# The gate projection of a linear-attention layer, from four passes of 512 columns to two blocks of 1024 columns with seven products on three of eight pairs

## The chip, the cores and the metric

The kernel is written for one Trainium2 chip and uses one of its cores. A core has five engines that matter here: TensorE (PE) multiplies matrices into a PSUM memory of eight banks, VectorE (DVE) and ScalarE (ACT) work on tiles in SBUF and PSUM, GpSimd (POOL) does small work and issues some of the DMAs, and SyncE (SP) issues the other DMAs. Each engine works through its own queue in order, and semaphores tie the queues together. The metric is the time of one execution on the device in microseconds (us). The kernel before took 2172.56 us as the median of three runs (2172.04 to 2177.0).

## The reference, cut to what matters

The program is a two-layer decoder on 256 positions of width 2048 in float32: a gated linear attention, a convolutional FFN, a block-sparse attention, and a second FFN. The change touches the first of these alone:

```python
xn = rms_norm(x, norm_w)
proj = xn @ w_in                       # 2048 -> q 1024, k 1024, v 2048, g 2048
q, k, v, g = jnp.split(proj, ...)
...                                    # decays, chunked linear attention -> o, 4 heads of 512
o = rms_norm(o, o_norm_w) * jax.nn.silu(g)      # the gate
return o.reshape(B, S, 2048) @ w_out
```

The gate is the last quarter of `proj`: 256 rows times a weight matrix of 2048 x 2048, whose result goes through SiLU and multiplies the normalized output of the attention.

## The kernel before, in words

**Products in three parts.** TensorE runs on a rounded float32 format. So that the result keeps float32's precision, each operand is split in a high and a low part, and each product is done three times: high times high, low times high, high times low. The activations are split once (`xw`). The weights come from HBM in tiles of 128 x 2048 (`wraw`, 1 MB each), and each half of 128 x 1024 is split when it is needed: ACT casts the high part (`whi`, line 150) and DVE subtracts to get the low part (`wlo`, line 152). A *step* is the work that TensorE does with one such half. `WeightStream.prefetch` emits the splits a few steps ahead of their use; `whi` and `wlo` live in three rotating buffers each (`parts`), and some of them in slots of a larger pool.

**Two ways to do a block.** `gemm_tok` is the plain way: 512 columns at a time, two accumulators in PSUM (one for each 128 rows), eight steps of 12 products of 512 columns each. `down` does 1024 columns at a time over eight *pairs* of 256 input features, and uses all eight PSUM banks. A plain pair there is two steps of 12 products. A pair that the table `ORDERS` marks with `+` is done by a Strassen-like scheme with seven block products in place of eight: 21 products of 512 columns in four steps (3, 6, 6 and 6). For such a pair DVE makes sums of the weights (`t13` and `t24`, lines 111 to 113), the sums are split too (3.5 halves in place of 2), and sums of the activations have to be there (`comb`). At the end of a block the partial results in the banks `p1` to `p8` are added up by one ACT copy and eight DVE additions. For names in `DIRECT` this is done between and after the last pairs, the tail: ACT copies `p1`, DVE adds `p6` and `p7`, then come the additions with `p2`, `p4`, `p5`, and after the second half of the tail those with `p3` and `p8`.

**The stage of the change.** The order is: values, keys (`down("k")`, one block, three of eight pairs by seven products), queries (two passes of `gemm_tok`), gate (four passes of `gemm_tok`, one for each head), then the output projection (`down("go")`). Inside the query and gate stages the attention itself is done: `gla_scores` (TensorE's `sT`) and `gla_values` (`o`) for each head. `after(n, job)` puts a job in front of the n-th next step. When a pass of the gate is done, ACT applies SiLU to the two accumulators, DVE multiplies with the normalized attention output and transposes 32 x 32 blocks (`z`), and GpSimd writes `z` to HBM and reads it back transposed (`turned`). Some steps later `gated` scales it (`g`), splits it (`go`) and, for pairs that the output projection does by seven products, makes operand sums (`comb`, lines 312 to 315); these four or five small operations are queued behind the split that was emitted last (`ws.behind()`).

**What sets the order.** The program is written with these jobs and due steps, and a scheduler then places the instructions of each engine's queue. So the order that the chip sees on each engine is that of the built program, of which the section on the change shows pieces.

## Time and profile before

| what | value |
|---|---|
| median of three runs | 2172.56 us (2172.04 to 2177.0) |
| the profiled execution, its own time | 2172.24 us |
| its span, first to last instruction | 2170.5 us |
| PE busy in the span | 2160.8 us |
| DVE, ACT busy in the span | 1639.0 us, 1294.7 us |
| TensorE's granted clock over the span | 1.00 |
| keys' block, 100.9 to 142.4 us: PE, DVE, ACT busy | all of it, 37.9, 26.5 us of 42.5 |
| gate stage with its attention, 203.0 to 290.3 us: PE, DVE, ACT busy | all of it, 51.0, 57.1 us of 87.3 |

The span is what the profiler records from the first to the last instruction; the execution's own time has 1.7 us around it. PE's busy time takes in overlapping, pipelined products, so that "busy" says that PE was not waiting, and how densely it works is read from the start of one product to the next. An idle time that the profile gives for an engine is the time just before an instruction, with the event that ended it.

### The profile page before, as it was taken

To read this page: it belongs to the slowest core of one execution; us is meant where nothing else is said; L and a number is where in the kernel's file an instruction comes from. 1 tells how busy PE (TensorE), PEld (TensorE's weight loads), DVE (VectorE), ACT (ScalarE), POOL (GpSimd) and SP (SyncE) were. 2 spreads that over 40 slices of the span, in tenths; PEclk is the share of its full clock that TensorE was granted. 3 is DMA by queue.
4 is the path that set the end of the run, shared out by engine and by line. 5 is a ranking of instruction groups with operands and counts; after the bars stand their busy time and mean duration, and the time that the engine had idled before them with its cause. 6 is when DMAs were issued, how large, how long until landed. Compare 5 with 4: busy or idle time off the path is not lost.

```text
span 2170.5 us, 27023 instructions
## 1 busy us (share of the span) xinstructions
PE 2160.8 (100%) x9681; PEld 1790.7 (83%) x9681; DVE 1639.0 (76%) x2274; ACT 1294.7 (60%) x1872; POOL 296.8 (14%) x448
## 2 busy tenths in 40 slices
PE   9999999999999999999999999999999999999999
PEld 7888888888888888888888888888888888888887
DVE  6785687667776767988977787676777776779987
ACT  6656665556555556555566676565656565656454
POOL 1011111111111111000022241011111111110000
PEclk9999999999999999999999999999999999999999
DMA  8566577677777777575676887676777778785655
GB/s 316 182 232 214 195 244 251 224 232 251 240 245 237 247 236 246 201 259 203 237 270 241 270 273 238 201 235 228 236 247 232 252 235 251 233 252 204 242 195 173
DMA packets 91480, 510.10 MB, mean 235 GB/s; under 512 B 13729, under 2 KB 14769, under 8 KB 41426
## 3 DMA queue, kind: packets, MB, share of 16 engines
q1 hardware_dynamic: 60722, 417.53, 55.2%
q0 software_dynamic: 30048, 90.28, 15.1%
q8 instruction: 75, 1.23, 0.2%
q10 hardware_dynamic: 576, 0.58, 0.1%
q14 instruction: 59, 0.48, 0.1%
HBM read 463.22 MB, written 45.11 MB: 234 GB/s over the span
## 4 chain that ended last, share of the span: by engine, by line
PE 94%; issue 3%; DMA 1%; ACT 0%; DVE 0%; SPq 0%; POOL 0%; DVEq 0%; POOLq 0%; ACTq 0%
PE acc L299 41%; PE p L353 31%; PE acc L302 20%; DMA w2s<-w2a 0%; PE hf L836 0%; DMA c<-rows 0%; PE sT L694 0%; PE o L711 0%; DMA wraw<-w_v 0%; PE s L949 0%; ACT whi L150 0%; DMA gn<-cst 0%; PE z L552 0%; PE s L947 0%; DVE wlo L152 0%
## 5 line engine op out<-in xcount | busy, mean ns | idle before, releaser
L152 DVE TENSOR_TENSOR wlo<-wraw,whi 128x1024 fp32r<-128x1024 f32 (+1 forms) x786 | 926.2, 1187 | 385.0 <-ACT whi L150 374.8
L150 ACT CAST whi<-wraw 128x1024 fp32r<-128x1024 f32 (+1 forms) x786 | 797.4, 1025 | 624.5 <-PE acc L299 394.7
L299 PE MATMUL acc<-whi,xw 128*128 128x512 f32 x3584 | 888.3, 390 | 2.4 <-ACT whi L150 2.1
L299 PEld LDWEIGHTS acc<-whi,xw 128*128 128x128 f32 x3584 | 671.4, 188 | 144.3 <-ACT whi L150 4.0
L302 PE MATMUL acc<-wlo,xw 128*128 128x512 f32 x1792 | 480.0, 389 | 0.0
L302 PEld LDWEIGHTS acc<-wlo,xw 128*128 128x128 f32 x1792 | 336.3, 188 | 69.9
L353 PE MATMUL p<-whi,hid 128*128 128x512 f32 x1078 | 288.1, 389 | 0.0
L353 PEld LDWEIGHTS p<-whi,hid 128*128 128x128 f32 x1078 | 202.2, 188 | 41.9
L353 PE MATMUL p<-wlo,hid 128*128 128x512 f32 x539 | 155.2, 389 | 0.0
L150 ACT CAST whi<-t 128x1024 fp32r<-128x1024 f32 x90 | 92.7, 1052 | 81.6 <-PE p L353 68.3
L780 POOL DMA_DIRECT2D upT<-turned x176 | 113.9, 654 | 144.8 <-DMA turned<-z 63.3
L299 PE MATMUL acc<-whi,xkv 128*128 128x512 f32 x512 | 127.9, 391 | 0.0
L774 POOL DMA_DIRECT2D turned<-z x44 | 34.1, 774 | 681.4 <-DVE z L770 618.0
L353 PEld LDWEIGHTS p<-wlo,hid 128*128 128x128 f32 x539 | 101.2, 188 | 21.1
L152 DVE TENSOR_TENSOR wlo<-t,whi 128x1024 fp32r<-128x1024 f32 x90 | 107.9, 1218 | 10.9 <-PE p L353 5.7
L353 PE MATMUL p<-whi,comb 128*128 128x512 f32 x360 | 116.1, 389 | 0.0
L789 ACT ACTIVATE au<-upT,cs 128x256 f32<-128x256 f32 x176 | 96.0, 595 | 23.8 <-DMA upT<-turned 23.7
L299 PEld LDWEIGHTS acc<-whi,xkv 128*128 128x128 f32 x512 | 94.6, 188 | 18.7
L793 DVE SCALAR_TENSOR_TENSOR au<-upT,cs,au 128x255 f32<-128x255 f32 x176 | 76.6, 470 | 12.8 <-ACT au L789 12.7
L795 DVE SCALAR_TENSOR_TENSOR au<-upT,cs,au 128x254 f32<-128x254 f32 x176 | 80.3, 476 | 0.0
L353 PEld LDWEIGHTS p<-whi,comb 128*128 128x128 f32 x360 | 67.5, 188 | 13.9
L302 PE MATMUL acc<-wlo,xkv 128*128 128x512 f32 x256 | 68.8, 390 | 0.0
(240 smaller groups left out, 1810.6 us busy)
## 6 DMA issues: line engine op xcount, KB each, us to landing
wraw<-w_up SPq DMA_DIRECT2D x176, 1024.0 KB, 5.3
wraw<-w_dn SPq DMA_DIRECT2D x88, 1024.0 KB, 4.9
turned<-z POOLq DMA_DIRECT2D x44, 512.0 KB, 3.5
upT<-turned POOLq DMA_DIRECT2D x176, 128.0 KB, 5.0
wraw<-w_g SPq DMA_DIRECT2D x16, 1024.0 KB, 5.0
wraw<-w_go SPq DMA_DIRECT2D x16, 1024.0 KB, 6.2
wraw<-w_kk SPq DMA_DIRECT2D x16, 1024.0 KB, 5.7
wraw<-w_kv SPq DMA_DIRECT2D x16, 1024.0 KB, 6.3
```

The lines of the kernel that those rows point to most:

```text
L150: one = nc.scalar.copy(hi[:, a:b], src[:, a:b])
L152: two = nc.vector.tensor_sub(lo[:, a:b], src[:, a:b], hi[:, a:b].bitcast(F32))
L299: T.matmul(ps[t], xs(kt)[:, x0 + 128 * t:x0 + 128 * t + 128], hi[:, c:c + 512], start=kt == 0 and x0 == 0, stop=False)
L302: T.matmul(ps[t], xs(kt)[:, 128 * t:128 * t + 128], lo[:, c:c + 512], start=False, stop=kt == KT - 1)
L353: T.matmul(p[n], x[xi], w[wi][:, 512 * f:512 * f + 512], start=n not in begun, stop=left[n] == 0)
L774: nc.gpsimd.dma_start(turned[J].rearrange("(a i) r q c -> (i r) a (q c)", a=4), z.rearrange("p (a q) t c -> p a (q t c)", a=4))
L780: nc.gpsimd.dma_start(f[32 * q:32 * q + 32].rearrange("p a (i c) -> p (a i) c", i=4), turned[J][:, :, q, :].rearrange("a r c -> r a c"))
L789: A.activation(au[:, i, :], t[:, i, :], AF.Identity, bias=col(cb + n), scale=col(cw + 2 * 2 * FT + n))
L793: V.scalar_tensor_tensor(au[:, i, 1:], t[:, i, :S - 1], col(cw + 2 * FT + n), au[:, i, 1:], op0=OP.mult, op1=OP.add)
L795: V.scalar_tensor_tensor(au[:, i, 2:], t[:, i, :S - 2], col(cw + n), au[:, i, 2:], op0=OP.mult, op1=OP.add)
```

## The change

The gate becomes a third user of `down`, as two blocks of 1024 columns. Pairs 1, 3 and 4 are done by seven products, after the plain pairs 0, 2 and 5; pairs 6 and 7 are the tail. The sums of the activations are those that the keys' block made (`x_sums`), which are kept. The function `gate` becomes `gate_rows`, which gets a finished tile in SBUF instead of an accumulator in PSUM. The due steps of the attention's scores and values move, so that they fall in plain pairs, where four PSUM banks are free, and those of `gated` move from 12 steps behind to 8 or 9. The weights of the gate are stored in the order of the new blocks.

```diff
+    "g": [_order("0 2 5 1+ 3+ 4+ | 6 7"), _order("0 2 5 1+ 3+ 4+ | 6 7")],
 }
-DIRECT = ("k", "mq")
+DIRECT = ("k", "mq", "g")
...
-    plan = [..., (w_qa, 2, 8192), (w_g, 4, 8192), (w_go, "go", None),
+    plan = [..., (w_qa, 2, 8192), (w_g, "g", None), (w_go, "go", None),
...
-    down("k", nrm.xs, {}, None, key_rows, {})
+    x_sums = {}
+    down("k", nrm.xs, x_sums, None, key_rows, {})
...
-            after(11 + 2 * i, lambda hd=hd: gla_scores(hd))
-            after(13 + 2 * i, lambda hd=hd: gla_values(hd))
+            after((10, 22)[g] + i, lambda hd=hd: gla_scores(hd))
+            after((12, 24)[g] + i, lambda hd=hd: gla_values(hd))
...
-    def gate(hd, ps):
-        z = fresh()
-        for t in range(2):
-            g = temp("tok", (128, 512))
-            A.activation(g, ps[t], AF.Silu, scale=nrm.col[:, t:t + 1])
-            V.scalar_tensor_tensor(g, heads[hd]["o"][:, t, :], heads[hd]["r"][:, t:t + 1], g,
-                                   op0=OP.mult, op1=OP.mult)
-            square(z, g, t)
-        return z
-
     fresh, square, through = turned("gates", GH)
-    for hd in range(GH):
-        z = gemm_tok(xs, 1, lambda ps: gate(hd, ps))
-        through(hd, z, [(12 + i, lambda f, c=2 * hd + i: gated(c, f)) for i in range(2)])
+    zg = {}
+
+    def gate_rows(t, hd, g):
+        if t == 0:
+            zg[hd] = fresh()
+        A.activation(g, g, AF.Silu, scale=nrm.col[:, t:t + 1])
+        V.scalar_tensor_tensor(g, heads[hd]["o"][:, t, :], heads[hd]["r"][:, t:t + 1], g, op0=OP.mult, op1=OP.mult)
+        square(zg[hd], g, t)
+        if t:
+            through(hd, zg[hd], [(8 + hd % 2 + i, lambda f, c=2 * hd + i: gated(c, f)) for i in range(2)])
+
+    down("g", nrm.xs, x_sums, None, gate_rows, {})
...
-        "w_g": _groups(win[:, 2 * KD + VD:], 512),
+        "w_g": _quads(win[:, 2 * KD + VD:], ORDERS["g"]),
```

A line is added at the top, so that the lines from 54 on stand one further down in the changed kernel, and those of the gate some more.

**First place: DVE's queue where the operands of the output projection's first pairs are made.** Before, this falls in the plain passes of the gate; these are the rows for head 1 (its third and fourth pair of columns, `go_2375` and `go_2397`).

```order
L152 TENSOR_TENSOR wlo_2339<-wraw_2239,whi_2338 128x1024
L152 TENSOR_TENSOR wlo_2355<-wraw_2239,whi_2354 128x1024
L152 TENSOR_TENSOR wlo_2379<-wraw_2273,whi_2378 128x1024
L314 TENSOR_TENSOR comb_2400<-g_2394 128x128
L312 TENSOR_TENSOR comb_2400<-g_2394 128x128
L428 TENSOR_TENSOR go_2375<-g_2372,go_2375 128x2x256
L313 TENSOR_TENSOR comb_2400<-comb_2400,g_2394 128x128
L428 TENSOR_TENSOR go_2397<-g_2394,go_2397 128x2x256
L315 TENSOR_TENSOR comb_2400<-g_2394,comb_2400 128x128
L152 TENSOR_TENSOR wlo_2409<-wraw_2273,whi_2408 128x1024
```

In the changed kernel the same work, here for head 0 (`go_2295`, `go_2309`), stands in the second block of the gate, between the splits and weight sums of its first two pairs with seven products.

```order
L153 TENSOR_TENSOR wlo_2277<-t13_2149,whi_2276 128x1024
L113 TENSOR_TENSOR t24_2272<-t13_2271,wraw_2082 128x512
L153 TENSOR_TENSOR wlo_2299<-t24_2150,whi_2298 128x1024
L315 TENSOR_TENSOR comb_2312<-g_2306 128x128
L114 TENSOR_TENSOR t24_2272<-wraw_2082,t24_2272 128x512
L313 TENSOR_TENSOR comb_2312<-g_2306 128x128
L429 TENSOR_TENSOR go_2295<-g_2292,go_2295 128x2x256
L153 TENSOR_TENSOR wlo_2321<-wraw_2082,whi_2320 128x512
L429 TENSOR_TENSOR go_2309<-g_2306,go_2309 128x2x256
L314 TENSOR_TENSOR comb_2312<-comb_2312,g_2306 128x128
L316 TENSOR_TENSOR comb_2312<-g_2306,comb_2312 128x128
L429 TENSOR_TENSOR comb_2317<-comb_2312,comb_2317 128x4x128
```

What moved: the small operations, which stood among splits of plain pairs, now stand among the splits and sums of `t13` and `t24`. Ahead of these rows DVE has `wlo_2254`, `t13_2271` and one scalar operation, and the half `whi_2330` comes next on ACT.

**Second place: ACT's queue for head 1's operands.** Before, with what each waits for:

```order
L617 ACTIVATE g_2372<-turned_2160,cs_82 128x256
L150 CAST whi_2378<-wraw_2273 128x1024 [waits DMAHW6_49,DVE_49,PE_49]
L617 ACTIVATE g_2394<-turned_2160,cs_82 128x256 x2
L428 CAST go_2375<-g_2372 128x2x256 [waits Activation_49]
L428 CAST go_2397<-g_2394 128x2x256 [waits Activation_49]
L150 CAST whi_2408<-wraw_2273 128x1024 [waits DVE_49,PE_49]
L428 CAST comb_2405<-comb_2400 128x4x128 [waits DVE_49]
L150 CAST whi_2419<-wraw_2319 128x1024 [waits DMAHW7_49,PE_49]
```

In the changed kernel these stand at the third pair with seven products of the second block; `whi_2387` and `whi_2397` are the first and second half of that pair, and `p1_2302` is the bank whose last product is the one with `whi_2387` and its low part.

```order
L151 CAST whi_2355<-t13_2271 128x1024 [waits PE_49]
L618 ACTIVATE g_2366<-turned_2192,cs_82 128x256 x2
L151 CAST whi_2380<-t24_2272 128x1024 [waits PE_49]
L151 CAST whi_2387<-wraw_2201 128x512 [waits DMAHW4_49,PE_49,Activation_49]
L428 CAST go_2347<-g_2344 128x2x256 [waits Activation_49]
L428 CAST go_2369<-g_2366 128x2x256 [waits Activation_49]
L406 COPY c0_2507<-p1_2302 128x512 [waits PE_49]
L428 CAST comb_2377<-comb_2372 128x4x128 [waits DVE_49]
L151 CAST whi_2397<-wraw_2201 128x1024
```

What moved: the copy of `p1` to SBUF, which the gate did not have, and the cast of the operand sums now stand ahead of the cast of the next half that TensorE needs.

**Third place: DVE's queue at the seam to the output projection.** Before, ten rows around the end of the last gate pass:

```order
L152 TENSOR_TENSOR wlo_2430<-wraw_2358,whi_2429 128x512
L113 TENSOR_TENSOR t24_2415<-wraw_2358,t24_2415 128x512
L152 TENSOR_TENSOR wlo_2446<-wraw_2358,whi_2445 128x1024
L152 TENSOR_TENSOR wlo_2469<-t13_2414,whi_2468 128x1024
L747 SCALAR_TENSOR_TENSOR tok_2485<-o_2074,r_o_2093,tok_2485 128x512
L747 SCALAR_TENSOR_TENSOR tok_2489<-o_2074,r_o_2093,tok_2489 128x512
L111 TENSOR_TENSOR t13_2463<-wraw_2427 128x1024
L112 TENSOR_TENSOR t24_2464<-t13_2463,wraw_2427 128x512
L508 STREAM_TRANSPOSE z_2484<-tok_2485 128x4x4x32
L508 STREAM_TRANSPOSE z_2484<-tok_2489 128x4x4x32
```

In the changed kernel, the rows from the first additions of the second block's tail on (`p5` to `p2` are its banks, `wraw_2440` is the first pair with seven products of the output projection):

```order
L414 TENSOR_TENSOR c1_2508<-c1_2508,p5_2336 128x512
L112 TENSOR_TENSOR t13_2464<-wraw_2440 128x1024
L409 TENSOR_TENSOR c0_2507<-c0_2507,p2_2115 128x512
L411 TENSOR_TENSOR c3_2510<-c2_2509,p4_2117 128x512
L113 TENSOR_TENSOR t24_2465<-t13_2464,wraw_2440 128x512
L153 TENSOR_TENSOR wlo_2474<-wraw_2401,whi_2473 128x1024
L414 TENSOR_TENSOR c2_2509<-c2_2509,p5_2336 128x512
L153 TENSOR_TENSOR wlo_2492<-wraw_2440,whi_2491 128x512
L114 TENSOR_TENSOR t24_2465<-wraw_2440,t24_2465 128x512
L751 SCALAR_TENSOR_TENSOR c0_2507<-o_2170,r_o_2189,c0_2507 128x512
L751 SCALAR_TENSOR_TENSOR c3_2510<-o_2170,r_o_2189,c3_2510 128x512
L417 TENSOR_TENSOR c1_2508<-c1_2508,p3_2116 128x512
```

What moved: eight additions, and the gating of two heads in place of one, now lie between the splits of the output projection's first pairs.

## Rows read from the trace of the kernel before

**Rows 1.** The page: busy time of each engine, share of the span, instructions.
```profile
PE 2160.8 (100%) x9681; PEld 1790.7 (83%) x9681; DVE 1639.0 (76%) x2274; ACT 1294.7 (60%) x1872; POOL 296.8 (14%) x448
```
**Rows 2.** What PE waited for in the whole span: total us, times, longest us.
```profile
PE acc L299 <- ACT whi L150: 2.1, 3, 1.3
PE hf L836 <- DVE c L420: 1.4, 1, 1.4
```
**Rows 3.** Stretches (keys' block, gate, output projection): length, busy us of PE to POOL, PEclk, DMA.
```profile
100.00:142.50 42.50, 42.50 (x190) 35.17 (x189) 37.92 (x44) 26.47 (x31) 0.61 (x1) 1.00 0.58 212
203.00:290.30 87.30, 87.30 (x416) 73.33 (x415) 50.95 (x72) 57.07 (x90) 11.11 (x19) 1.00 0.57 193
290.30:335.00 44.70, 44.70 (x201) 36.97 (x200) 35.96 (x42) 27.00 (x40) 7.51 (x11) 1.00 0.76 244
```
**Rows 4.** The chain that ended last, the keys' block: start us, us, what.
```profile
100.94 41.48 PE p L353 x183
```
**Rows 5.** DVE's groups by form: busy us, mean ns of one, idle before and releaser.
```profile
L152 DVE TENSOR_TENSOR wlo<-wraw,whi 128x1024 fp32r<-128x1024 f32 x737 | 895.4, 1221 | 383.3 <-ACT whi L150 374.3 <-PE p L353 3.9 <-PE acc L302 2.1
L111 DVE TENSOR_TENSOR t<-wraw 128x1024 f32<-128x1024 f32 x45 | 54.9, 1220 | 11.4 <-DMA wraw<-w_go 4.3 <-DMA wraw<-w_dn 4.3 <-DMA wraw<-w_mo 2.4
L152 DVE TENSOR_TENSOR wlo<-wraw,whi 128x512 fp32r<-128x512 f32 x49 | 33.4, 684 | 1.7 <-PE p L353 0.9 <-ACT whi L150 0.4 <-PE acc L302 0.2
L420 DVE TENSOR_TENSOR c<-c,p 128x512 f32<-128x512 f32 x32 | 20.9, 682 | 33.0 <-DMA c<-rows 14.7 <-PE p L353 14.3 <-DMA c<-x_tok 3.8
L508 DVE STREAM_TRANSPOSE z<-tok 128x512 f32<-128x512 f32 x12 | 8.1, 695 | 0.0
L747 DVE SCALAR_TENSOR_TENSOR tok<-o,r_o,tok 128x512 f32<-128x512 f32 x8 | 5.6, 744 | 1.7 <-ACT tok L746 1.7
L428 DVE TENSOR_TENSOR go<-g,go 128x512 fp32r<-128x512 f32 x8 | 5.4, 681 | 0.0
```
**Rows 6.** DVE in order of time, head 0's operands in the gate: start us, us, what.
```profile
257.84 1.22 DVE L152 TENSOR_TENSOR wlo<-wraw,whi 128x1024 fp32r<-128x1024 f32 x1 [1.49 <-ACT whi L150]
258.98 0.28 DVE L314 TENSOR_TENSOR comb<-g 128x128 f32<-128x128 f32 x1
259.18 0.28 DVE L312 TENSOR_TENSOR comb<-g 128x128 f32<-128x128 f32 x1
```
**Rows 7.** ACT in order of time, parts of the gate and of the output projection.
```profile
203.22 0.59 ACT L712 COPY o<-o 128x512 f32<-128x512 f32 x1 [1.21 <-PE o L711]
...
204.35 0.58 ACT L712 COPY o<-o 128x512 f32<-128x512 f32 x1
...
258.52 1.13 ACT L427 CAST go<-g 128x512 fp32r<-128x512 f32 x2
259.55 1.05 ACT L150 CAST whi<-wraw 128x1024 fp32r<-128x1024 f32 x1
...
306.62 0.59 ACT L383 COPY c<-p 128x512 f32<-128x512 f32 x1 [3.17 <-PE p L353]
307.11 1.06 ACT L150 CAST whi<-wraw 128x1024 fp32r<-128x1024 f32 x1
```
**Rows 8.** PE in order of time, at the start of the program: after a wait, and without.
```profile
12.75 2.11 PE L299 MATMUL acc<-whi,xw 128*128 128x512 f32 x8 [1.28 <-ACT whi L150]
...
18.34 1.98 PE L299 MATMUL acc<-whi,xw 128*128 128x512 f32 x8
```
**Rows 9.** POOL in order of time, head 3's way through HBM.
```profile
299.15 0.56 POOL L511 DMA_DIRECT2D gates<-z  x1 [15.94 <-DVE z L508]
302.61 2.18 POOL L517 DMA_DIRECT2D turned<-gates  x4 [2.90 <-PE p L353]
```
**Rows 10.** DMA issues: engine, times, KB each, median us to landing.
```profile
wraw<-w_g SPq DMA_DIRECT2D x16, 1024.0 KB, 5.0
wraw<-w_go SPq DMA_DIRECT2D x16, 1024.0 KB, 6.2
turned<-gates POOLq DMA_DIRECT2D x16, 128.0 KB, 5.7
```

More of the change, by code (lines that the diff above doesn't have):

```diff
@@ L195, in trunk @@
     ws = WeightStream(tc, raw, parts)
-    plan = [(w_v2, 1, 16384), (w_v, 2, 8192), (w_k, "k", None), (w_qa, 2, 8192), (w_g, 4, 8192), (w_go, "go", None),
+    plan = [(w_v2, 1, 16384), (w_v, 2, 8192), (w_k, "k", None), (w_qa, 2, 8192), (w_g, "g", None), (w_go, "go", None),
             (w_up0, FT // 2, 8192), (w_dn0, "dn0", None),
```

## The prediction

> **What bounds the kernel now.** I read the busy times first: PE is busy for all but 10 us of the span [rows 1]. PE's waits sum to a few us, none over 1.4 us, and none lies in the stage of the change [rows 2]. [...] The chain of waits then gives PE's pace: 183 products of 512 columns in 41.48 us, 0.2267 us each, with nothing between them [rows 4]. So a product that goes is worth 0.2267 us as long as DVE and ACT keep ahead, and the question is whether they do.
>
> **What the change removes.** Before, the gate is 4 passes of 8 steps of 12 products, 384. After, each block has 3 pairs of 21 and 5 of 24, 183 products, and two blocks 366. 18 products x 0.2267 = 4.1 us off PE. The attention's own products are the same and only move.
>
> **What it adds on DVE and ACT.** By the rows' durations an operation of 1024 columns takes DVE 1.22 us, one of 512 columns 0.68, and the next starts 0.08 earlier than that (0.28 us long and 0.20 from start to start) [rows 5, 6]. I count start to start: 1.14 and 0.60, 0.20 for a `comb` operation, 0.66 for the gating (L747), 0.62 for a transpose. A pair by seven products costs DVE three sums (1.14 + 0.60 + 0.60) and splits of 3.5 halves (3 x 1.14 + 0.60), 6.4 us, in PE's 21 x 0.2267 = 4.8. A plain pair costs it 2.3 us in 5.4. The keys' block alternates them at first and has two in a row; here three stand in a row, 19.1 us of DVE in 14.3 us of PE. On top come 16 additions out of PSUM, 16 x 0.60 = 9.6 us. ACT gets 1.5 casts more per such pair and two copies. No operand sums are made for the gate, since those of the keys stay.
>
> For the additions the row shows 682 ns from PSUM (L420) against 681 from SBUF (L428) [rows 5]. [...]
>
> **First block: nothing lost.** The six plain steps before its first pair by seven give DVE room, with only the scores, the values and the queries' operations there. Running down its queue in the built order I find the low parts of the three pairs ready 0.5 us or more before PE comes to them. If that cover is gone, it costs what is missing, up to the deficit of the second block. PSUM: the second block's first four banks are freed by the copy of `p1` and the additions with `p6`, `p7` and `p2`, all done some 3 us before they are wanted.
>
> **Second block: three waits.** Here the operands of heads 0 and 1 come back from HBM just when the pairs by seven are split (first and second place of the change).
> *A.* From the last product of head 3's first half on, PE has 45 products (rest of the values 4, of the plain pair 1 + 4 + 12, first pair by seven 21, half step 3), 45 x 0.2267 = 10.2 us, until it wants `whi_2330`. The other way there: the product's tail 0.16 (390 ns less the pace), ACT's copy and square 1.13 (203.22 to 204.35) [rows 7], the cast of `whi_2253` 1.05, then on DVE four operations of 1024 columns, five of 512, four of `comb` and a small one, 4.6 + 3.0 + 0.8 + 0.1 = 8.5, then ACT's cast of the operand sums 0.53 and of `whi_2330` 1.05. Sum 12.4: a wait of 2.2 us.
> *Between.* From there to the low part of `whi_2387` DVE has four of 1024, two of 512 and two of `comb`, 6.2 us, and PE 20 products, 4.5: 1.6 us.
> *B.* The last product into `p1` needs that low part. `whi_2397`, which PE wants next, stands on ACT behind the copy of `p1` and behind the cast of the operand sums, and these wait for DVE's next five operations (three of 512, two of `comb`, 2.3 us with the last one's tail). 2.3 + 0.53 + 1.05 less one product, 0.2: 3.6 us. Were DVE not late, the wait would still be 0.16 + 0.49 (306.62 to 307.11) + 0.53 + 1.05 = 2.2 us [rows 7].
> *C.* From there to the second half of the output projection's second plain step DVE has no pause: 13 low parts and 2 sums of 1024, 12 operations of 512, four gatings, three transposes: 17.1 + 7.2 + 2.6 + 1.9 = 28.8 us. PE has 119 products in that time, 27.0. That is 1.8 us, if the weights are there. Before, `w_go` took 6.2 us to land against 5.0 for `w_g`, and DVE waited 4.3 us for it [rows 5, 10]; a transfer that comes too late makes C up to 4. I take 2.6.
> *D.* Head 3's way through HBM. Its transposes end some 14.7 us after the block's end, 53 products and C's wait further; store 0.3 + 3.5 [rows 9], loads 1.6 + 5.7 [rows 9, 10], and ACT's four scalings, `p1` copy, casts, 4.2: 30.0. PE comes to `whi_2746` after 126 products and C, some 30.5. So nothing at the median; loads 2.5 us later than that would cost 2. I take 0.5.
>
> Each wait also restarts PE's pipeline: eight products took 2.11 us after a wait and 1.98 without [rows 8]; 8 waits, 1.0 us.
>
> **Sum.** 2.2 + 1.6 + 3.6 + 2.6 + 0.5 + 1.0 = 11.5 us lost, 4.1 won, 7.4 longer. Against the profiled execution's own 2172.24 us (span 2170.5) that is 2179.6; the median of the runs is 0.3 us above that execution, so 2180.0. The range for this case: with C at 1.8, D at 0 and A gone it is 2176, with B at its least and no other change 2178.6, with C at 4, D at 2 and a first block that loses 2 us 2185.
>
> **Rivals.**
> *The helpers keep up.* In the keys' block DVE works 89% of the time and PE doesn't wait [rows 3, 4]; if the queues run as well here, A, the piece between, C and D fall away, since each is one long sum against another. B cannot fall below 2.2 by the order of ACT's queue unless `p1` is ready before the cast would start, which it isn't, as its last product is the one before. So 2172.56 - 4.1 + 2.2 = 2170.7, or 2168.4 if even B hides. It decides at A: where `whi_2330` starts 2.2 us earlier than summed, nothing accumulates behind it. For it speaks PE's unbroken pace before; against it DVE's 28.8 us of queue in 27.0 of PE, which no order can hide.
> *Only B and C remain*, as A's start lies earlier than summed: 3.6 + 1.8 + 0.5 - 4.1 = 1.8 us longer, 2174.4.
> *The transfers decide.* Pairs by seven eat 1 MB of weights in 4.8 us where plain ones take 5.4, while loads take 5.0 to 6.2 us to land [rows 10]. With `raw` of three tiles, a tile comes free only when its sums and splits are made, so a late DVE makes the next load late too. At 1 us for each of the six pairs it would be 2186. DMA queues' share was 0.57 in the gate and 0.76 in the output projection [rows 3], which leaves room.
> *The clock falls.* Before, no wait of PE was over 1.4 us and the granted clock stayed at 1.00 [rows 2, 3]; B is a longer wait than any that this trace has. [...]
>
> **Chances.** Forecast 0.58 (2176 to 2185, most of it near 2180); only B and C 0.19; helpers keep up 0.13; transfers 0.06; clock 0.04. About 0.3%, 6.5 us, is what a measurement of this kernel can tell from no change. Slower by more than that begins at 2179.1: some three quarters of the forecast (0.44), transfers and clock (0.10), 0.54. Faster by more would need 6.5 us, more than the 4.1 that are removed: 0.04 for what I overlook. Within: 0.42. The range that leaves out 2 in 10 reaches from 2169.5, inside the case that the helpers keep up, to 2187.
>
> **What would show it.** Right: PE with 366 products in the gate's two blocks at 0.227 us and no wait before the second block's pairs by seven; then waits there for ACT's `whi`, the longest one on the first wide half of the third pair, behind the copy of `p1`; DVE without a pause over the seam, and a wait for `wlo` in the output projection's first pair by seven. Wrong: no wait in the second block (the sums A and B are then off), waits in the first block or for PSUM banks at the seam between the blocks, or a clock under 1.00. The forecast as a whole is wrong if the waits between the gate's start and the output projection's end sum to under 6 us or over 18.

## The result and the profile after

The changed kernel takes 2186.08 us (median of 6 runs, 2182.02 to 2187.92) against 2172.3 us (6 runs) for the kernel before: a ratio of 1.0053, with a 95% interval from 1.0043 to 1.0063. That is 13.8 us more by the medians and 11.5 by the ratio, against a forecast of 7.4. The profiled execution is the longest of the six, 2187.92 us with a span of 2186.1, 15.7 us longer than the profiled one before; the costs below are those of this execution. The six times go with the clock: the mean granted clock is 0.997 in the three longest, 0.998 in the next two and 0.999 in the shortest.

The page's busy times of the changed kernel (to be read beside [rows 1]):

```profile
PE 2165.7 (99%) x9663; PEld 1791.1 (82%) x9663; DVE 1671.4 (76%) x2320; ACT 1301.6 (60%) x1884; POOL 298.9 (14%) x448
```

PE has the 18 products less that were counted. DVE has 46 instructions and 32 us more. What PE waited for (total us, times, longest us; of before in [rows 2]):

```profile
PE p L354 <- ACT whi L151: 11.5, 5, 4.7
PE hf L837 <- DVE c L421: 1.3, 2, 0.7
```

The same stretches as in [rows 3], the gate's end and the output projection's moved to where they now lie (length, busy us of PE to POOL, PEclk, DMA share, GB/s):

```profile
100.00:142.50 42.50, 42.50 (x189) 35.21 (x188) 37.90 (x45) 26.25 (x32) 0.61 (x1) 1.00 0.57 211
203.00:296.00 93.00, 86.78 (x386) 70.38 (x385) 78.88 (x108) 62.78 (x100) 9.64 (x14) 0.96 0.54 178
296.00:345.00 49.00, 44.34 (x188) 35.99 (x187) 34.67 (x42) 25.97 (x38) 10.28 (x16) 0.93 0.77 231
```

The keys' block is as it was. In the gate DVE has 78.9 us of work where it had 51.0, PE stands still for 6.2 us, and the granted clock is 0.96, no longer 1.00. PE in order of time (start us, us, what, idle before and what ended it) has four stops of over 0.5 us for ACT's high parts up to 345 us, three in the second block and one in the output projection:

```profile
268.13 0.50 PE L354 MATMUL p<-whi,comb 128*128 128x512 f32 x1 [2.23 <-ACT whi L151]
...
271.63 0.50 PE L354 MATMUL p<-whi,comb 128*128 128x512 f32 x1 [0.56 <-ACT whi L151]
...
278.21 0.79 PE L354 MATMUL p<-whi,comb 128*128 128x512 f32 x1 [3.30 <-ACT whi L151]
...
329.50 5.83 PE L354 MATMUL p<-whi,go 128*128 128x512 f32 x13 [4.66 <-ACT whi L151]
```

The last row says a second thing: 13 products in 5.83 us, where eight take 1.98 [rows 8]. The stretches behind the third and the fourth stop (columns as above):

```profile
278.20:283.90 5.70, 5.69 (x13) 4.46 (x14) 5.70 (x5) 4.79 (x5) 0.00 (x0) 0.50 0.54 184
329.40:335.00 5.60, 5.50 (x13) 4.34 (x14) 5.60 (x7) 3.84 (x5) 2.69 (x4) 0.50 0.70 116
```

The granted clock is 0.50 in both. 13 products would take 2.95 us at 0.2267; from start to start they take 5.70 and 5.67, which is 2.75 and 2.72 us more.

**Where the time went.** The gate's first product starts at 185.78 us before and 185.21 after (the table and [rows 3], which take the gate from 203.0 on, leave its first 17 us out). The output projection's first starts at 290.10 and 295.97, the FFN's at 377.14 and 391.73. So the gate takes 104.3 us before and 110.8 after, 6.4 more. With the 4.1 us of removed products 10.5 were lost: 6.1 in the three stops, 2.75 in the half clock, and the rest, 1.7, in restarts and short waits. The output projection takes 87.0 and 95.8 us, 8.7 more: 4.66 at the fourth stop, 2.72 in the half clock, 0.7 for the turn (`hf`, where PE transposes finished sums of the output projection), and 0.6 in restarts. All else differs by under 1 us in sum.

ACT ahead of the first stop:

```profile
266.51 0.62 ACT L428 CAST comb<-comb 128x512 fp32r<-128x512 f32 x1 [2.60 <-DVE comb L316]
267.04 1.04 ACT L151 CAST whi<-wraw 128x1024 fp32r<-128x1024 f32 x1
```

The cast that PE waits for stands behind the cast of the operand sums, and that one waited 2.60 us for DVE. ACT around the third stop:

```profile
272.00 1.14 ACT L428 CAST go<-g 128x512 fp32r<-128x512 f32 x2
274.94 0.59 ACT L406 COPY c<-p 128x512 f32<-128x512 f32 x1 [1.81 <-PE p L354]
276.59 0.62 ACT L428 CAST comb<-comb 128x512 fp32r<-128x512 f32 x1 [1.06 <-DVE comb L316]
277.12 1.04 ACT L151 CAST whi<-wraw 128x1024 fp32r<-128x1024 f32 x1
```

Here the cast that PE needs stands behind the copy of `p1` as well, and the cast of the operand sums again waits for DVE. The fourth stop, on ACT and on POOL:

```profile
315.38 1.06 ACT L151 CAST whi<-wraw 128x1024 fp32r<-128x1024 f32 x1 [0.49 <-DMA wraw<-w_go]
325.29 1.70 ACT L618 ACTIVATE g<-turned,cs 128x256 f32<-128x256 f32 x4 [8.85 <-DMA turned<-gates]
326.90 0.56 ACT L384 COPY c<-p 128x512 f32<-128x512 f32 x1
327.36 1.14 ACT L428 CAST go<-g 128x512 fp32r<-128x512 f32 x2
328.40 1.99 ACT L151 CAST whi<-wraw 128x1024 fp32r<-128x1024 f32 x2
```
```profile
308.86 0.56 POOL L512 DMA_DIRECT2D gates<-z  x1 [2.78 <-DVE z L509]
312.36 2.19 POOL L518 DMA_DIRECT2D turned<-gates  x4 [2.95 <-ACT whi L151]
```

Head 3's loads are issued from 312.36 us on, 16.4 us behind the seam, and ACT gets them at 325.29. The landing times, of heads 2's and 3's loads after, then of all heads' before:

```profile
DMA to landing us min/median/max: 3.5/5.3/11.3
```
```profile
DMA to landing us min/median/max: 3.1/5.7/8.4
```

The 8.4 us before is head 3's too: its four loads took 4.5, 7.4, 7.5 and 8.4 us there, and 7.0, 10.6, 11.2 and 11.3 after.

### The profile page after: what moved, and what is told of

It is laid out like the page before. It is cut to its first block, busy times and chain, and to the rows that moved or that the text cites. A ratio compares the mean times of both kernels' runs of the same rounds, so it can differ in the third digit from the quotient of the medians.

```text
span 2186.1 us, 27044 instructions
## 1 busy us (share of the span) xinstructions
PE 2165.7 (99%) x9663; PEld 1791.1 (82%) x9663; DVE 1671.4 (76%) x2320; ACT 1301.6 (60%) x1884; POOL 298.9 (14%) x448
## 3 DMA queue, kind: packets, MB, share of 16 engines
q0 software_dynamic: 30048, 90.28, 15.1%
## 4 chain that ended last, share of the span: by engine, by line
PE 83%; DMA 2%; DVE 1%; issue 1%; ACT 0%; POOL 0%; DVEq 0%; ACTq 0%; POOLq 0%
PE acc L300 36%; PE p L354 28%; PE acc L303 18%; DMA turned<-gates 1%; DMA wraw<-w_mo 1%; DVE wlo L153 0%; PE hf L837 0%; DMA wraw<-w_dn 0%; PE s L950 0%; ACT whi L151 0%; DVE t L112 0%; PE o L499 0%; PE s L948 0%; DMA gates<-z 0%; POOL turned L518 0%
## 5 line engine op out<-in xcount | busy, mean ns | idle before, releaser
L300 PE MATMUL acc<-whi,xw 128*128 128x512 f32 x3328 | 824.2, 390 | 1.4 <-ACT whi L151 1.1
L300 PEld LDWEIGHTS acc<-whi,xw 128*128 128x128 f32 x3328 | 624.3, 188 | 133.0 <-ACT whi L151 2.6
L303 PE MATMUL acc<-wlo,xw 128*128 128x512 f32 x1664 | 445.8, 389 | 0.0
L303 PEld LDWEIGHTS acc<-wlo,xw 128*128 128x128 f32 x1664 | 312.6, 188 | 64.9
L151 ACT CAST whi<-t 128x1024 fp32r<-128x1024 f32 x102 | 105.4, 1053 | 80.7 <-PE p L354 66.5
L354 PE MATMUL p<-whi,comb 128*128 128x512 f32 x408 | 134.6, 395 | 6.8 <-ACT whi L151 6.8
L153 DVE TENSOR_TENSOR wlo<-t,whi 128x1024 fp32r<-128x1024 f32 x102 | 122.4, 1220 | 9.8 <-PE p L354 5.2
L354 PE MATMUL p<-whi,xw 128*128 128x512 f32 x412 | 110.5, 392 | 0.0
L354 PEld LDWEIGHTS p<-whi,comb 128*128 128x128 f32 x408 | 77.4, 190 | 24.7 <-ACT whi L151 8.7
L354 PEld LDWEIGHTS p<-whi,xw 128*128 128x128 f32 x412 | 77.8, 189 | 16.1
```

Of the source, the lines that this page charges most:

```text
L151: one = nc.scalar.copy(hi[:, a:b], src[:, a:b])
L153: two = nc.vector.tensor_sub(lo[:, a:b], src[:, a:b], hi[:, a:b].bitcast(F32))
L300: T.matmul(ps[t], xs(kt)[:, x0 + 128 * t:x0 + 128 * t + 128], hi[:, c:c + 512], start=kt == 0 and x0 == 0, stop=False)
L303: T.matmul(ps[t], xs(kt)[:, 128 * t:128 * t + 128], lo[:, c:c + 512], start=False, stop=kt == KT - 1)
L354: T.matmul(p[n], x[xi], w[wi][:, 512 * f:512 * f + 512], start=n not in begun, stop=left[n] == 0)
```

## The experiments

Ratios are to runs of the kernel before on the same chip in the same job (its medians in the four jobs: 2173.4, 2174.2, 2174.2 and 2173.2 us). Idle times are of each kernel's profiled execution.

**One pair by seven in the second block.**

```diff
-    "g": [_order("0 2 5 1+ 3+ 4+ | 6 7"), _order("0 2 5 1+ 3+ 4+ | 6 7")],
+    "g": [_order("0 2 5 1+ 3+ 4+ | 6 7"), _order("0 2 5 1+ 3 4 | 6 7")],
```

> The second block does one pair by seven products in place of three: 6 products more than the changed kernel (372 in the gate, 12 fewer than before, 2.7 us), and 2 x (6.4 - 2.3) = 8.2 us less DVE work. Theory (DVE's and ACT's queues are too late in the second block): the waits of 2.2, 0.6 and 3.3 us for whi and the half clock behind the last are gone, so that the output projection starts at 287.4 to 289 us of the span (295.97 in the changed kernel, 290.10 before). Head 3's wait in the output projection (4.7 us there) gets smaller, since DVE reaches the seam earlier, but some may stay: 2170 to 2176 us. Rival (weight transfers are what is late): the loads come at the same pace, so waits of 4 us or more stay in the second block, and the time is 2181 us or more.

Measured: 1.0020 (1.0011 to 1.0028), a median of 2177.9 us. All of PE's stops between the gate's start and 325 us:

```profile
299.37 1.20 PE L354 MATMUL p<-wlo,go 128*128 128x512 f32 x4 [0.54 <-DVE wlo L153]
318.72 3.92 PE L354 MATMUL p<-whi,go 128*128 128x512 f32 x9 [2.49 <-ACT whi L151]
```

The second block has none. The gate's weights took 4.8 us from issue to landing at the median in the changed kernel and 5.0 before [rows 10], so they were not what was late: DVE's and ACT's queues were. The wait for head 3 is halved and still costs, with a clock of 0.57 in the 4 us behind it. The time is above the range that was expected, 2170 to 2176. Not all of that is the seam: the profiled execution, 2180.41 us, reaches the FFN 3.3 us later than before and loses the rest further on, with a second stop of 1.8 us for `whi` and a mean clock of 0.998 over the execution.

**The operands of heads 0 and 1 put off.**

```diff
-            through(hd, zg[hd], [(8 + hd % 2 + i, lambda f, c=2 * hd + i: gated(c, f)) for i in range(2)])
+            lags = ((18, 20), (20, 22), (8, 9), (9, 10))[hd]
+            through(hd, zg[hd], [(lags[i], lambda f, c=2 * hd + i: gated(c, f)) for i in range(2)])
```

> The scaling, splitting and operand sums for heads 0 and 1 are put off by some ten steps, behind the second block's three pairs by seven, to its last plain pairs and the first steps of the output projection; the three pairs in a row stay. Theory (that work is what makes DVE late): the first two waits of the second block go to under 1 us in sum and the third falls from 3.3 to about 1.2 us, with the clock at 1.00 there; but DVE, without a pause over the seam already, gets 5.2 us more there, so that waits of 3 to 8 us for wlo and whi show in the output projection's first pairs: 2178 to 2186 us. Rival (only the place beside the pairs by seven hurts, and the seam has room): no new wait in the output projection, 2173 to 2176 us. Second rival (three pairs by seven in a row are too much by themselves, 19.1 us of DVE in 14.3 of PE): waits of 4 us or more stay in the second block.

Measured: 1.0038 (1.0026 to 1.0050), 2182.07 us. PE's stops in the second block and the output projection:

```profile
274.30 0.50 PE L354 MATMUL p<-whi,comb 128*128 128x512 f32 x1 [0.84 <-ACT whi L151]
...
297.48 0.79 PE L354 MATMUL p<-wlo,comb 128*128 128x512 f32 x1 [2.68 <-DVE wlo L153]
...
302.81 0.50 PE L354 MATMUL p<-wlo,comb 128*128 128x512 f32 x1 [0.48 <-DVE wlo L153]
...
305.53 1.20 PE L354 MATMUL p<-wlo,go 128*128 128x512 f32 x4 [1.51 <-DVE wlo L153]
...
310.27 4.33 PE L354 MATMUL p<-whi,go 128*128 128x512 f32 x10 [3.54 <-ACT whi L151]
```

Three pairs by seven in a row make 0.84 us of stops by themselves; the rest of the 6.1 us came from what was queued among them. Put off, that work makes 8.2 us of stops at the seam, where DVE has no pause either. The debt is moved, not paid.

**Zero products while PE would wait.** `none` is a tile of zeros, `w_last` the high part of the weights in use.

```diff
+            def fill(n, x, times):
+                for _ in range(times):
+                    T.matmul(p[n][:32], none, x, start=False, stop=False)
...
+                    if name == "g" and b == 1 and k == 4:
+                        fill(5, w_last[0], 12)
...
+                    if name == "go" and b == 0 and f == 0 and i == 1:
+                        fill(2, w_last[0], 18)
```

> TensorE gets products with a zero operand to do while it would wait: 12 of 512 columns behind the first two products into p1 of the second block's third pair by seven, and 18 ahead of pair 6 in the output projection's first block, where it waits for head 3. They add zero to a bank, so nothing else changes; 12 x 0.2267 = 2.7 us and 18 x 0.2267 = 4.1 us, each shorter than the time that TensorE stood there (3.3 and 4.7 us). Theory (the clock falls because TensorE stands still): the granted clock stays at 1.00 at both places, and the 13 products behind each wait go from 0.43 to 0.2267 us, 2 x 2.6 = 5.2 us less; up to 2.5 us of the first gain comes back as waits for wlo at the start of the output projection, where DVE has no pause. So 2181 to 2184 us. Rival (the clock falls for another reason, or DVE's queue decides all of it): 2186 to 2188 us.

Measured: 1.0096 (1.0083 to 1.0109), 2194.92 us, slower than either theory said. At the place of the third stop it did what was meant (PE's rows, then the stretches behind the first and the third stop):

```profile
268.07 0.80 PE L362 MATMUL p<-whi,comb 128*128 128x512 f32 x1 [2.23 <-ACT whi L151]
...
278.15 0.50 PE L362 MATMUL p<-whi,comb 128*128 128x512 f32 x1 [0.73 <-ACT whi L151]
...
305.20 0.50 PE L362 MATMUL p<-wlo,comb 128*128 128x512 f32 x1 [0.64 <-DVE wlo L153]
...
306.93 1.20 PE L362 MATMUL p<-wlo,go 128*128 128x512 f32 x4 [0.52 <-DVE wlo L153]
```
```profile
268.00:271.40 3.40, 3.33 (x8) 2.69 (x9) 3.35 (x3) 3.40 (x7) 0.00 (x0) 0.50 0.31 65
278.10:283.80 5.70, 5.65 (x25) 4.56 (x26) 5.67 (x5) 5.70 (x8) 0.00 (x0) 1.00 0.53 187
```

The half `whi` comes at 278.15, as without the fill (278.21), PE stood for 0.73 us and not 3.30, and the clock behind it is 1.00: 25 products in 5.7 us in place of 13. Behind the first stop, which was not filled, the clock is 0.50 here. Part of it comes back as waits for `wlo` at the seam, 1.2 us, as expected. The sum failed, for a reason beside the question. With the products the order at the seam was built otherwise: POOL issued head 3's loads only at 318.30, released by an ACT cast, so that the 18 products did not fit into the wait but came on top of it (2.58 us more at 331.22), and a wait of 4.58 us for the turn followed, where DVE's additions stood behind a weight sum that waited 4.1 us for its tile. So this run shows what the clock does at one place, in one execution, and nothing about the total.

**Head 3 without its loads.**

```diff
-            after(fetch, lambda: got.update(f=load(g)))
+            if name == "gates" and g == 3:
+                got = seen[2]
+            else:
+                after(fetch, lambda: got.update(f=load(g)))
+            seen[g] = got
```

> Head 3's way back from HBM is left out: its four loads are dropped, and its scaling takes head 2's tile in place of its own, so that this part of the computation is changed. The store stays. Theory (head 3's loads, which land 11.3 us after their issue, are the only thing that pair 6 of the output projection waits for): the wait of 4.7 us and the half clock behind it (2.7 us more for 13 products) go, 7.4 us less: 2178 to 2180 us, with the waits in the gate's second block as they are. Rival (the weight tile of pair 6, which landed 11.1 us after its issue, or ACT's queue would be late anyway): 2 us or more of the wait stay and the clock may still fall: 2182 to 2186 us.

Measured: 1.0037 (1.0025 to 1.0049), 2182.01 us. The stops of 2.22 and 3.31 us in the second block stay, the fourth one is gone. But two waits for `wlo`, 0.8 and 2.3 us, come up in the output projection's second block, behind weight sums that wait 3.1 and 2.5 us for their tiles. Of the 7.4 us expected some 4 are gained (3.5 by the ratios, 4.0 in the length of the output projection): further on the transfers of the weights are near. The time lies at the rival's lower edge, 2182, but not for its reason, since nothing of the fourth wait stayed.

**Only the first block by the block scheme.**

```diff
-    "g": [_order("0 2 5 1+ 3+ 4+ | 6 7"), _order("0 2 5 1+ 3+ 4+ | 6 7")],
+    "g": [_order("0 2 5 1+ 3+ 4+ | 6 7")],
...
+    for hd in (2, 3):
+        z = gemm_tok(xs, 1, lambda ps: gate(hd, ps))
+        through(hd, z, [(12 + i, lambda f, c=2 * hd + i: gated(c, f)) for i in range(2)])
```

> Only the gate's first block of 1024 columns (heads 0 and 1) is done by the block scheme, with its three pairs by seven; heads 2 and 3 are two plain passes as in the kernel before, with the old lags for their way through HBM. 375 products, 9 fewer than before, 2.0 us. Theory (the first block costs nothing, all of the loss is that heads 0 and 1 return into the second block's pairs by seven and that heads 2 and 3 end together): no wait of TensorE over 0.3 us between the gate's start and the FFN, and a time 2.0 us below the kernel before, a ratio of 0.999. Rival (DVE's debt from the pairs by seven is carried on, or the block scheme costs by itself): waits behind the first block, and a ratio of 1.000 or more.

Measured: 1.0001 (0.9992 to 1.0011). PE does not wait in the gate at all and the clock stays at 1.00, so the first block is free, as forecast. But the 2.0 us come back in the output projection. PE, and DVE before it:

```profile
331.54 0.44 PE L851 MATMUL hf<-mk,c 128*128 128x128 f32 x2 [1.76 <-DVE c L421]
```
```profile
329.67 1.23 DVE L112 TENSOR_TENSOR t<-wraw 128x1024 f32<-128x1024 f32 x1 [7.78 <-DMA wraw<-w_go]
330.81 1.28 DVE L421 TENSOR_TENSOR c<-c,p 128x512 f32<-128x512 f32 x2
```

The additions that PE's turn waits for stand behind a weight sum whose tile lands late. Half of the theory (the first block) holds, the forecast of the time does not.

**One pair by seven, head 3's pairs one step later.** The first kernel above, and

```diff
-    "go": [_order("0 1+ 2 3+ 4 | 5 6 7"), ...
+    "go": [_order("0 1+ 2 3+ 4 5 | 6 7"), ...
...
-    middle("go", go, go_sums, from_input, n_ffn, rows1, TURNS, True)
+    middle("go", go, go_sums, from_input, n_ffn, rows1, ((0, (1, 1)),) * 2 + TURNS[2:], True)
```

The second part fits the place of the first two turns to the shorter tail.

> The kernel with one pair by seven in the second block, and the output projection's first block has pairs 6 and 7 (head 3) one step later: pair 5 stands before the tail, and the tail has two pairs. One step is 12 products, 2.72 us. Theory (head 3's operands come a fixed time after the seam): the wait of 2.5 us for them there goes to zero and so does the half clock behind it (3.4 us at half rate, 1.7 us); 4.2 us less than that kernel's 4.3 us over the kernel before: within 1.5 us of the kernel before. Rival (the loads come later by as much, because they share the queues with the weights): the wait stays at 1.5 us or more.

Measured: 1.0012 (1.0000 to 1.0023). The wait goes from 2.49 to 1.81 us only, and the eight products behind it take 3.33 us, where eight take 1.98 [rows 8]:

```profile
318.31 3.33 PE L354 MATMUL p<-whi,go 128*128 128x512 f32 x8 [1.81 <-ACT whi L151]
```

That is the rival's number, but not its reason: the loads are no later, 8.7 us to landing at most where the kernel above has 9.1. On ACT the cast that PE waits for stands behind head 3's scalings, the last of which starts at 315.3 us, when the loads have landed. The next experiment has the same.

**The same order in the changed kernel.**

> The changed kernel with the same order of the output projection's first block, head 3's pairs one step of 2.72 us later. Theory: the wait before pair 6 goes from 4.7 to about 2 us, and with it in some executions the half clock (up to 2.7 us): 2180.5 to 2183.5 us in the terms of the first comparison, 1.0035 to 1.005 times the kernel before. Rival (a later use moves the loads too): no change, a ratio of 1.0055 to 1.0065. The waits in the gate's second block stay as they are by both.

Measured: 1.0061 (1.0046 to 1.0077); the theory is wrong, and so is the rival's reason. PE's stop:

```profile
329.87 3.66 PE L354 MATMUL p<-whi,go 128*128 128x512 f32 x8 [4.63 <-ACT whi L151]
```

It is as long as before (4.66) and now stands before the second step of pair 5, which needs nothing of head 3. The built order of ACT's queue says why; `whi_2746` is that step's half:

```
L151 CAST whi_2730<-wraw_2630 128x1024
L618 ACTIVATE g_2724<-turned_2621,cs_82 128x256 x2
L618 ACTIVATE g_2740<-turned_2621,cs_82 128x256 x2
L384 COPY c0_2768<-p1_2632 128x512
L428 CAST go_2727<-g_2724 128x2x256
L428 CAST go_2743<-g_2740 128x2x256
L151 CAST whi_2746<-wraw_2630 128x1024
```

The cast is queued behind head 3's scalings, which wait for the loads, and the loads did not move: the last of the scalings starts at 326.9 us, in the changed kernel at 326.5, and the last load took 11.3 us in both.

**Half of three weight tiles.**

```diff
-            for a, b in self.cuts.get(self.n_dma, ((0, n),)):
+            for a, b in self.cuts.get(self.n_dma, ((0, 1024 if self.n_dma in self.half else n),)):
...
-            src = ... self.tiles[c][:, o:o + 1024]
+            src = ... self.tiles[c][:, 0 if c in self.half else o:][:, :1024]
...
+    ws.half = {at + 5, at + 6, at + 7}
```

> Of the weight tiles of pairs 5, 6 and 7 in the output projection's first block only half is loaded (512 KB each), and that half is used twice, so that this part of the computation is changed. Everything else is the changed kernel's. Theory (head 3's loads take 11.3 us because they share the DMA engines with these tiles, which are issued 2.1 and 0.3 us ahead of them): 1 MB less moves in 310 to 325 us, the loads land in 5 to 8 us, and the wait before pair 6 goes from 4.7 us to under 2 us. Rival (the loads are slow by themselves, or what is late is only the issue, 18 us after the seam): they still take 10 us or more, and the wait stays above 3.5 us.

Measured: 1.0038 (1.0024 to 1.0052), 2182.49 us. The landing times of heads 2's and 3's loads:

```profile
DMA to landing us min/median/max: 3.4/4.5/5.7
```

5.7 us at most, where they took 11.3; the stop before pair 6 is gone, and the stops of 2.23 and 3.20 us in the second block stay. So the loads were slow because of the weight tiles' bytes that moved beside them.

**Head 3 behind the casts.** The kernel with pair 5 ahead of the tail, and

```diff
+            lags = ((8, 9), (9, 10), (8, 9), (13, 14))[hd]
```

> As the kernel with pair 5 ahead of the tail (head 3's pairs one step later), and head 3's scaling and splitting are put off by four more steps, so that on ScalarE the casts for the two steps of pair 5 and for pair 6 stand ahead of them. Theory (in that kernel TensorE waited 4.6 us for a cast which needs nothing of head 3, but stood behind head 3's scalings in ScalarE's queue): the wait moves one step on, to the first product with head 3's own operand, and shrinks to 2 us or less; 1.0035 to 1.005 times the kernel before, where that kernel had 1.0061. Rival (the weight tiles of pairs 5 and 6, late by the crowded transfers, are what the cast waits for): a wait of 3 us or more stays, for a cast behind a DMA, and the time is that of that kernel within 0.1%. The waits of 2.2, 0.6 and 3.3 us in the gate's second block stay by both.

Measured: 1.0031 (1.0019 to 1.0043), against 1.0061 without this line. PE's stops from the gate's start to the FFN are those of the second block, and the output projection has none:

```profile
269.29 0.50 PE L354 MATMUL p<-whi,comb 128*128 128x512 f32 x1 [2.23 <-ACT whi L151]
...
272.78 0.50 PE L354 MATMUL p<-whi,comb 128*128 128x512 f32 x1 [0.55 <-ACT whi L151]
...
279.36 0.80 PE L354 MATMUL p<-whi,comb 128*128 128x512 f32 x1 [3.30 <-ACT whi L151]
```
```profile
290.00:384.50 94.50, 94.50 (x429) 78.05 (x428) 80.00 (x97) 56.19 (x83) 16.06 (x24) 1.00 0.78 254
```

So this kernel prices the gate nearly alone: 0.0031 x 2174 = 6.7 us, beside the 6.4 that the gate lost above.

**Two ways to keep the first block's gain.** The first block alone, with the first two turns later in the output projection; and the first block alone, with plain pair 4 ahead of the pairs by seven in the output projection's second block.

```diff
-    middle("go", go, go_sums, from_input, n_ffn, rows1, TURNS, True)
+    middle("go", go, go_sums, from_input, n_ffn, rows1, ((1, 1),) * 2 + TURNS[2:], True)
```
```diff
-    "go": [..., _order("0 2 1+ 3+ 4 | 5 6 7")],
+    "go": [..., _order("0 2 4 1+ 3+ | 5 6 7")],
```

> The kernel with the first block alone by the block scheme, whose 2.0 us came back as waits of 1.8 and 1.3 us for the sums that are turned in the output projection. Here the first two of these turns stand 5 to 6 steps later, in the middle of the output projection's second block. Theory (the gain is lost only at that wait): the wait of 1.8 us goes, nothing else moves, and the ratio to the kernel before is 0.9985 to 0.9995. Rival (from 305 to 325 us the transfers run at a share of 1.0, so that what is won ahead of them is waited for behind them, wherever TensorE is held): another wait takes its place, and the ratio stays at 0.9995 to 1.001.

> Again the first block alone by the block scheme; in the output projection's second block the plain pair 4 stands ahead of the two pairs by seven, so that VectorE's weight sums, which waited 7.8 us for their tile with the additions for the turn queued behind them, come 2.7 us later in the program and behind these additions. Theory (the turn was late through VectorE's queue): the wait of 1.8 us goes without moving the turn, ratio 0.9985 to 0.9995. Rival (the transfers hold the stage): a wait for a weight tile or for the residual in its place, ratio 0.9995 to 1.001.

Measured: 0.9989 (0.9980 to 0.9999) for both, medians of 2172.83 and 2172.09 us beside 2174.17. In both the wait of 1.76 us for the turn is gone. In the first, small waits of 0.5, 0.2 and 0.6 us take part of its place; in the second none does (what PE waited for in the whole span):

```profile
PE acc L300 <- ACT whi L151: 3.0, 4, 1.4
PE junk L223 <- POOL idle L220: 1.3, 1, 1.3
PE hf L851 <- DVE c L421: 0.6, 1, 0.6
```

Both beat the kernel before by 0.1%, at the edge of what can be told. The kernel before with the mended order alone was not run, so it stays open how much of this is owed to the nine products.

**All mends together.** Both blocks by the block scheme with one pair by seven in the second, head 3 behind the casts and one step later, and the output projection's second order from the last kernel.

> Both of the gate's blocks by the block scheme, with one pair by seven in the second (372 products, 12 fewer than before, 2.7 us), head 3's pairs one step later in the output projection and its scaling behind the casts, and the plain pair 4 ahead of the pairs by seven in the output projection's second block. Theory (each wait was named rightly, and the mends add up): no wait over 0.6 us for whi or wlo from the gate's start to the end of the output projection, clock 1.00 there, and a time of the kernel before less 2.7 us plus about 1 us of small waits at the seam: ratio 0.9985 to 0.9998. Rival (the output projection's transfers hold the stage, so that nothing more than the first block's gain can be had): another wait there, ratio 0.9998 to 1.001.

Measured: 0.9998 (0.9986 to 1.0010), 2173.74 us beside 2173.16. PE's stops from the gate's start to the FFN, for `wlo` at the seam and for head 3's operand:

```profile
299.72 1.20 PE L354 MATMUL p<-wlo,go 128*128 128x512 f32 x4 [0.54 <-DVE wlo L153]
...
320.01 3.01 PE L354 MATMUL p<-whi,go 128*128 128x512 f32 x12 [0.71 <-ACT go L428]
```

The clock is 1.00, and the profiled execution reaches the FFN at 376.14 us, 1.0 us ahead of before. The long waits are mended, but no gain is measured: the interval holds both what was expected and the rival.

## Why the prediction was right, and where it failed

*Removed work:* right. 18 products at 0.2267, 4.1 us.

*First block:* right. Nothing is lost there, in the changed kernel or with that block alone.

*A, between, B:* A and B right in place, cause and size: 2.2 and 3.6 were summed, 2.23 and 3.30 us measured. Between them 1.6 was summed for DVE's queue; the one stop there is 0.56 us and for ACT's cast, but from start to start PE lost 1.7 us, the rest in shorter waits. With fewer pairs by seven the stops go, with the operands put off they shrink to 0.84. The additions out of PSUM cost what the rows said: the next row is one of them, 684 ns beside 686 for the 512-column splits out of SBUF.

```profile
L408 DVE TENSOR_TENSOR c<-c,p 128x512 f32<-128x512 f32 x4 | 2.7, 684 | 0.1
```

*C:* the step failed, 2.6 us forecast, no stop measured. DVE's queue was counted rightly: from 278.19 to 307.9 it worked 28.8 us, with 0.9 of idle time. What was wrong is PE's side. Its 119 products took 29.8 us and not 27.0, since 13 of them ran at half clock, and so DVE was just in time:

```profile
308.00 1.19 PE L354 MATMUL p<-wlo,go 128*128 128x512 f32 x4
```

This is the place, the second plain step's low part; the row starts 0.47 us behind the two products before it (307.53), which is their own pace. Where the clock held at B (the zero products), 1.2 us of it were seen, though there the order at the seam was another. So on these numbers C and the half clock at B are not two costs to be added: the one hides the other.

*D:* the mis-sized term, 0.5 us forecast, 4.66 measured, outside the bound of 2. The transposes ended 12.6 us behind the seam (14.7 forecast, with C's wait in it), ACT needed 4.2 us (4.2), and the last load took 11.3 in place of the median of 5.7 [rows 10]. PE came after 28.9 us (30.5 forecast, where its own 126 products and 2.6 for C make 31.2). So the loads are what was wrong. The DMA share is 1.02 from 310 to 320 us, two weight tiles were issued 2.1 and 0.3 us ahead of the loads, and halving three tiles took the loads to 5.7 us and the wait to zero. That DVE's lateness is what brought tiles and loads together was not tested: before, the share is 1.0 from 305 us on too, and head 3's last load took 8.4 us. That row was there to be read, and 2.7 us above the median it is by the forecast's own working a wait of 2. Another part of the reason was missed altogether: on ACT the casts for the next weights stand behind the scalings that wait for the loads, so that a use later in PE's order doesn't help (4.63 us), and a place later in ACT's order does (none).

*The clock:* its falling was given a chance of 0.04, and it fell at two places in the changed kernel, to 0.50 behind stops of 3.30 and 4.66 us, which cost 2.75 and 2.72 us. It belonged in the sum. The trace of before has it at 1.00 in all three stretches [rows 3], so nothing measured stood behind the 0.04; these two places were the first to show what a fall costs. A clock under 1.00 was also named as a sign of being wrong, and it came. The forecast itself had waits of 2.2 and 3.6 us, beyond the 1.4 of any wait of before, so its own argument (B is longer than any wait of that trace) left the clock's price unknown, not nil.

*The sum:* forecast 10.5 us of waits and 1.0 for restarts; measured 6.1 + 4.7 us of stops, 0.7 for the turn, and 2.3 for restarts and short waits. That the waits agree is partly luck, C too large and D too small. What the forecast lacked is the half clock, 5.5 us: with it 7.4 become 12.9, and the two stages of the profiled execution lost 15.1. The median, 2186.08 us, lies above the forecast case's own range of 2176 to 2185 and inside the wider one, 2169.5 to 2187. It is also the number of the rival "the transfers decide", 2186, but that one was right at one place only, D, and there for the loads of an activation, not for the pairs by seven as it had it. "The helpers keep up" fell at A.

## What to carry to other kernels

When a change fills the engines that feed TensorE, find what falls due in the same stretch: three pairs by seven made 0.84 us of stops, and 6.1 with another job's operands among them. A wait that is forecast longer than any in the trace must be priced with the clock behind it (2.75 and 2.72 us here, behind 3.30 and 4.66), and a clock that falls may hide the next wait (C, 2.6 us forecast and no stop measured). For an operand that returns from HBM in several loads, take the last of its own loads in the trace (8.4 us before) and not the median of all (5.7). Look also at what is queued behind its first reader on that engine: moving its use left the wait as it was (4.66 and 4.63 us), moving that reader took 4.6 us of wait away.

## What the runs showed of the hardware that was not expected

- The granted clock fell to 0.50 behind PE's stops of 3.2 to 3.3 us in the second block in all five kernels that kept them (the changed one, head 3 without loads, head 3 later, half tiles, head 3 behind the casts; 0.51 over 3.4 us in the second of these). Behind the stop of 2.2 us ahead of it, it fell in four of six executions, to 0.50 in three and 0.58 over 3.9 us in one. The length of a stop alone does not tell: behind one of 1.81 us (one pair by seven, head 3's pairs one step later) eight products took 3.33 us in place of 1.98, and behind one of 2.58 (zero products, at 331 us) the clock stayed at 1.00. Where the gap of 3.3 us was filled to 0.73 us with zero products, it stayed at 1.00.
- Loads of 128 KB landed up to 11.3 us after their issue beside weight tiles at a DMA share of 1.02, and 5.7 us at most with half of the bytes of three of those tiles.
- The output projection gives a gain made ahead of it back where its tiles are late: with the first block alone DVE waited 7.78 us for one, and PE 1.76 and 1.3 us for the turns behind it.
